# The first block's tile arithmetic on GpSimd, written for VectorE and ScalarE instead

## The chip, the core and the metric

The kernel runs on one core of a Trainium2 chip. A core has TensorE (PE in the profile, its weight loads PEld), VectorE (DVE), ScalarE (ACT), GpSimd (POOL) and SyncE (SP, which here only issues DMAs). The metric is the device time of one execution in microseconds (us); lower is better. The kernel before took 3381.39 us, the median of 3 runs (3380.52 to 3383.11).

## The reference

Two blocks follow each other on a sequence of 1024 tokens of width 1024, in float32.

```python
# first block (one layer)
hx = modulate(rmsnorm(x), sh1, sc1); hc = modulate(rmsnorm(ctx), csh1, csc1)
aq, ak, av, mq, mk, mv, mo, gates = split(h @ w_in)           # for hx and for hc
att = latent_attention(rope(norm(aq)), rope(norm(ak)), av, cak, cav, sink)  # window 128, 8 heads
h_sum = bidir_mlstm(silu(conv(mq)), silu(conv(mk)), mv, ...)  # 4 heads, chunks of 128, two directions
mix = concat([att, rmsnorm(h_sum) * norm_w * sigmoid(mo)])
x = x + g1 * (mix @ w_out)
x = x + g2 * expert_choice_ffn(modulate(rmsnorm(x), sh2, sc2))  # 16 experts, 128 tokens each
# second block: an even layer (pooling, spatial gate) and an odd layer (dilated attention, gated conv), final rmsnorm
return rmsnorm(odd_layer(even_layer(x)))
```

The change touches what stands up to `x = x + g1 * (mix @ w_out)`, and the norm and modulation behind it; here that part is called the mixer. Experts and second block stay as they are.

## The kernel before

A float32 product is made of three matmuls: each operand is split into a high part, rounded to the type fp32r (`hi`, a copy on ACT), and the rest (`lo`, a subtraction), and `mm3` (L156 to L162) adds hi·hi, lo·hi and hi·lo. So weights that arrive from DRAM in `raw` need one cast on ACT (L148) and one subtraction, `lo_sub` (L134 on POOL, L136 on DVE), before TensorE can use them. `wchunk` does both; it takes its engine from `lo_engines`, which `run` sets to `["pool"]` (L204). There are 2 buffers of `raw` and 3 each of `hi` and `lo` in the mixer.

The mixer runs in this order:

- `h_all` (L340): normed rows are transposed, then `finish` (L361) makes hi and lo of `hx`, the modulated input; `kv_tile` projects attention keys, values and gates.
- `keys`, `gates`, `ctx_heads`, `proj_q` (L423 to L683): keys and queries are normed (`qk_norm`, L450), rotated (`rope`, L462), doubled (`qd`, L440 and L675) and transposed. `gates` is a long chain of small DVE instructions (L488 to L606).
- Four mLSTM heads: `head_qk`, `head_vo` project (weights by `wchunk`); `head_states` (L725) walks over the chunks for the states `C`; `head_chunks` (L752) makes, for each of 8 chunks, weights `W = exp(E + g)`, a product, and the normed output `hs` (L786, L787). The mask is added to `E` once for 4 chunks (L767).
- `mod_sums` (L314) adds up the modulation vectors in `macc` (L328, DVE), a DMA of `mraw` for each of its steps, spread between the heads.
- `attention` (L805): the fourth head's chunks run between the first attention blocks. `att_scores` (L891) makes a softmax in `P` for four heads of a group and scales each by `rl` (L933 for the first on POOL, L935 on DVE for the others); `att_values` (L938) transposes and multiplies; `out_tile` (L965) applies `w_out` (weights `wo`, scaled by `g1` at L838), adds the residual, norms and routes.

The program's source doesn't fix the order of the instructions: a scheduler (the tile layer's, with `high_priority` for the chunks) orders them for each engine when the program is built, and each engine then runs its own list strictly in that order. Where an instruction changes its engine, the lists of the others can move as well.

```python
    def lo_sub(self, lo, raw, hi, eng=None):
        ...
        if eng == "pool":
            nc.gpsimd.tensor_sub(lo, raw, hi.bitcast(F32))
        else:
            nc.vector.tensor_sub(lo, raw, hi.bitcast(F32))
```

Of the kernel before, what the change touches and what calls it, by code (L numbers as in the profile page):

```python
# [19 lines left out]
P = 128  # L20
# [62 lines left out]
class K:  # L83
# [115 lines left out]
    def run(self):  # L199
        tc = self.tc  # L200
        with ExitStack() as es:
            self.cpool = es.enter_context(tc.tile_pool(name="const", bufs=1))
            self.dram = es.enter_context(tc.tile_pool(name="dram", bufs=1, space=DRAM))
            self.lo_engines = ["pool"]  # L204
            self.const()
            for ph in (self.mixer, self.moe, self.even, self.odd):
                ph()
                if self.stop == ph.__name__:
                    return
# [131 lines left out]
    def h_all(self):  # L341
        nc, A = self.nc, self.A
        self.hx = ([self.t("hx", [D], F32R, "hxh") for _ in range(KT)], [self.t("hx", [D], F32R, "hxl") for _ in range(KT)])
        hc = [self.t("X", [4, 256], F32R, "hc") for _ in range(4)]
        self.hc = ([hc[k // 4][:, k % 4, :] for k in range(KT)], [hc[2 + k // 4][:, k % 4, :] for k in range(KT)])
        xnT = self.t("xnT", [KT, D])
        self.jtag = "tmp"

        def normed(src, t0, n):
            ts = []  # L350
            ss, rs = self.t("ss", [n]), self.t("ss", [n])
            for i in range(n):
                t = self.t("xin", [D])
                nc.sync.dma_start(t, A[src][(t0 + i) * P:(t0 + i + 1) * P, :])
                ts.append(t)
            self.norm_rows(ts, rs, ss)
            for i in range(n):
                nc.vector.tensor_scalar_mul(ts[i], ts[i], rs[:, i:i + 1])
            return ts

        def finish(h, l, src, kt, a):  # L361
            sc, sh = self.sc1[:, a, kt:kt + 1], self.sh1[:, a, kt:kt + 1]
            tmp = self.t("tmp", [h.shape[-1]])
            nc.scalar.activation(h, src, AF.Identity, scale=sc, bias=sh)  # L364
            nc.vector.tensor_scalar(tmp, src, sc, sh, op0=ALU.mult, op1=ALU.add)
            self.lo_sub(l, tmp, h, ("pool", "dve")[kt % 2])

        for t0 in range(8):
            for t in normed("x", t0, 1):
                for hf in range(2):  # L370
                    ps = self.pt("tr")
                    for k in range(4):
                        kt = hf * 4 + k
                        nc.tensor.transpose(ps[:, k * P:(k + 1) * P], t[:, kt * P:(kt + 1) * P], self.ident)
                    o = xnT[:, hf * 4:hf * 4 + 4, t0 * P:(t0 + 1) * P]
                    pv = ps.rearrange("p (a b) -> p a b", a=4)
                    if hf == 0:
                        nc.scalar.copy(o, pv)
                    else:
                        nc.vector.tensor_copy(o, pv)  # L380
        self.mod_early()
        self.kv_open()
        for hf in range(2):
            s = slice(hf * 512, hf * 512 + 512)
            for kt in range(KT):
                finish(self.hx[0][kt][:, s], self.hx[1][kt][:, s], xnT[:, kt, s], kt, 0)
            for t in range(4):
                self.kv_tile(hf * 4 + t)
        ts = normed("ctx", 0, 2)
        for kt in range(KT):  # L390
            ps = self.pt("tr")
            for i, t in enumerate(ts):
                nc.tensor.transpose(ps[:, i * P:(i + 1) * P], t[:, kt * P:(kt + 1) * P], self.ident)
            finish(self.hc[0][kt], self.hc[1][kt], ps[:, :256], kt, 1)
        for t in range(2):
            self.kv_tile(8 + t)
# [25 lines left out]
    def keys(self):  # L422

        nc, A, mp = self.nc, self.A, self.mp
        kx, kc = self.ktok, self.kct
        self.rt = self.t("rt", [8, 2, 32])
        nc.sync.dma_start(self.rt.rearrange("p t a d -> p (t a d)"), A["cst"][:, CST["rope"]])
        kr = self.t("k", [8, P], name="kr")
        self.qk_norm(kx.rearrange("p a (b c) -> p (a b) c", c=64), 1, kr)
        self.rope(kr, kx, 2)  # L430
        self.qk_norm(kc.rearrange("p a (b c) -> p (a b) c", c=64), 1, self.t("c1", [2, P], name="ksq"))
        self.dump("akr", kr)
        self.dump("kc", kc)
        kcc = mp.tile([P, 4, 256], F32R, name="kcc")
        self.kc = [(kcc[:, 2 * v], kcc[:, 2 * v + 1]) for v in range(2)]
        self.kx = [[mp.tile([P, D], F32R, name=f"kx{v}{i}") for i in range(2)] for v in range(2)]
        for src, t0 in [(kr, t) for t in range(0, 8, 2)] + [(kc, 0)]:
            kd = self.t("qd", [4, 2, 64])
            kv = src[:, t0:t0 + 2].rearrange("p t (v d) -> p (t v) d", v=2)
            nc.gpsimd.tensor_copy(kd, kv[:, :, None, :].to_broadcast([P, 4, 2, 64]))  # L440
            ps = self.pt("tr")
            for v in range(2):
                for t in range(2):
                    c = (v * 2 + t) * P
                    nc.tensor.transpose(ps[:, c:c + P], kd[:, t * 2 + v].rearrange("p a d -> p (a d)"), self.ident)
            for v in range(2):
                o = self.kc[v] if src is kc else [x[:, t0 * P:t0 * P + 256] for x in self.kx[v]]
                self.split2(o[0], o[1], ps[:, v * 256:(v + 1) * 256])

    def qk_norm(self, x, which, sq):  # L450
# [6 lines left out]
        nc.vector.tensor_reduce(ss, sq, axis=AX.X, op=ALU.add)  # L457
        self.rstd(rs, ss, 1.0 / 64)
        nc.vector.tensor_mul(x, x, rs[:, :, None].to_broadcast([P, n, 64]))
        nc.gpsimd.tensor_mul(x, x, self.qkn[:, which:which + 1, :].to_broadcast([P, n, 64]))  # L460

    def rope(self, out, x, nh, t0=0):  # L462

# [6 lines left out]
        o = out.rearrange("p t (h a d) -> p t h a d", a=2, d=32)  # L470
        for i, op in ((0, ALU.subtract), (1, ALU.add)):
            tmp = self.t("rtmp", [nt * nh, 32]).rearrange("p (t h) d -> p t h d", t=nt)
            nc.gpsimd.tensor_mul(o[:, :, :, i], v[:, :, :, i], cos)
            nc.vector.tensor_mul(tmp, v[:, :, :, 1 - i], sin)
            nc.vector.tensor_tensor(o[:, :, :, i], o[:, :, :, i], tmp, op=op)

# [223 lines left out]
    def head_vo(self, h):  # L700
# [6 lines left out]
        for t in range(0, 8, 2):  # L707
# [5 lines left out]
            nc.scalar.activation(so[:, t:t + 2], pv[:, :, 128:256], AF.Sigmoid)  # L713
            if t == 4:
                next(self.mod, None)
        nc.gpsimd.tensor_mul(so, so, nw[:, None, :].to_broadcast([P, 8, P]))
        return vo, so

    def head(self, h, hd):
# [32 lines left out]
    def head_chunks(self, h, hd, C, hook=None):  # L752
# [5 lines left out]
        for c in range(8):  # L758
            if hook:
                hook(c)  # L760
            if c % 4 == 0:

                E = self.t("E", [4, 2, P])
                src = self.mdr.rearrange("(c h) x -> h c x", h=4)[h][c:c + 4]
                ev = E.rearrange("p c d t -> p c (d t)")
                nc.sync.dma_start(ev, src[None].to_broadcast([P, 4, 256]))
                nc.gpsimd.tensor_add(ev, ev, self.mmask[:, None, :].to_broadcast([P, 4, 256]))  # L767
            s = slice(c * P, (c + 1) * P)
            pq = self.pt("s")
            nc.tensor.matmul(pq[:, :P], kT[:, s], qT[:, s], start=True, stop=True)  # L770
# [12 lines left out]
            nc.vector.scalar_tensor_tensor(den[:, 0], it[:, :, 128], -1.0, it[:, :, 128], op0=ALU.mult, op1=ALU.max)  # L783
            nc.vector.tensor_tensor(den[:, 0], den[:, 0], self.flo[:, :, c, h], op=ALU.max)
            nc.vector.reciprocal(den[:, 1], den[:, 0])
            nc.gpsimd.tensor_scalar(hs[:, c], it[:, 0, :P], den[:, 1, 0:1], None, op0=ALU.mult)  # L786
            nc.vector.scalar_tensor_tensor(hs[:, c], it[:, 1, :P], den[:, 1, 1:2], hs[:, c], op0=ALU.mult, op1=ALU.add)  # L787
            pool, n, bufs = self.tags["hj"]
            junk = pool.tile([P, P], BF16, tag="hj", name=self.nm("hj"), bufs=bufs)
# [2 lines left out]
        rs = self.t("hss", [8])  # L792
        self.rstd(rs, ss, 1.0 / P, "hrst")
        nc.vector.tensor_mul(hs, hs, rs[:, :, None].to_broadcast([P, 8, P]))
        nc.gpsimd.tensor_mul(hs, hs, so)
        for hf in range(2):
            ps = self.pt("tr")
            for t in range(4):
# [6 lines left out]
    def attention(self, last, right):  # L805
        nc, A, tc = self.nc, self.A, self.tc
        with ExitStack() as es:
# [3 lines left out]
            self.open(hp, "m2h", {"C3": (2080, 1), "kt3": (512, 2), "kw3": (128, 3)})  # L811
            self.banks(es, "m2l", {"sl": 1, "sc": 1, "O": 1})
            self.sls = ["sl"]
            self.npool = 1
            self.am = self.t("am", [640])
            nc.sync.dma_start(self.am[:, :384], A["cst"][:, CST["amask"]])
            nc.gpsimd.memset(self.am[:, 384:], 0.0)
# [15 lines left out]
            def weights(c, tag):  # L833
                hi, lo = self.t(tag, [2, D], F32R), self.t(tag, [2, D], F32R)
                for k in range(2):
                    raw = self.t("x1", [D])
                    nc.sync.dma_start(raw, A["wout"][c][:, k * D:(k + 1) * D])
                    nc.gpsimd.tensor_mul(raw, raw, g1)  # L838
                    nc.scalar.copy(hi[:, k], raw)
                    self.lo_sub(lo[:, k], raw, hi[:, k], "dve" if c > 1 else "pool")  # L840
                    self.wo.append((hi[:, k], lo[:, k]))

            def hook(c):
# [51 lines left out]
    def att_scores(self, v, b):  # L895
# [33 lines left out]
        nc.vector.tensor_add(l, l, es)  # L929
        nc.vector.reciprocal(rl, l)  # L930
        for g in range(4):
            if g < self.npool:
                nc.gpsimd.tensor_scalar(Ps[g], Ps[g], rl[:, g:g + 1], None, op0=ALU.mult)  # L933
            else:
                nc.vector.tensor_scalar_mul(Ps[g], Ps[g], rl[:, g:g + 1])  # L935
        return Ps
# [28 lines left out]
    def out_tile(self, b, at):  # L965
# [3 lines left out]
        raw, hm = self.t("hraw", [4, P]), self.t("hm", [2, 4, P], F32R)  # L969
        nc.sync.dma_start(raw, self.mixT.rearrange("(k p) t -> p k t", p=P)[:, :, r])  # L970
        nc.scalar.copy(hm[:, 0], raw)
        nc.gpsimd.tensor_sub(hm[:, 1], raw, hm[:, 0].bitcast(F32))
        m = [(at[0][:, k], at[1][:, k]) for k in range(4)] + [(hm[:, 0, k], hm[:, 1, k]) for k in range(4)]
        x = self.t("x1", [D])
        nc.sync.dma_start(x, A["x"][r, :])
# [22 lines left out]
        self.norm_rows([x], rs, ss)  # L998
        h2 = self.t("h2", [D])
        nc.vector.scalar_tensor_tensor(h2, x, rs, self.scb, op0=ALU.mult, op1=ALU.mult)  # L1000
        nc.gpsimd.tensor_add(h2, h2, self.shb)
        store(self.h2d[r, :], h2)
        st, lg, ex = self.t("sm", [4]), self.t("sm", [16]), self.t("sm", [16])
        nc.vector.scalar_tensor_tensor(lg, pl, rs, self.rsh, op0=ALU.mult, op1=ALU.add)
# [921 lines left out]
```

## Time and profile before

| | |
|---|---|
| median of 3 runs | 3381.39 us (3380.52 to 3383.11) |
| the profiled execution | 3381.84 us, of which the span from first to last instruction is 3379.7 us |
| busy: PE, DVE, ACT, POOL | 92%, 60%, 40%, 44% of the span |
| mean granted TensorE clock | 0.96 of full speed |
| the mixer | from 0 to about 803.5 us of the span |
| routing, experts | about 803.5 to 1180 us, then the second block |

The profile gives, for each engine, the time in which an instruction ran. Groups of instructions have one line each: line of the source, engine, operation, what it writes and reads, shapes and count, then busy time and mean duration of one in ns, then the idle time of the engine before them and what ended it. A wait is put down to the instruction that ended it last. [...]

### The profile page before, as it was taken

How to read it: one execution, taken by the hardware profiler on the slowest of the kernel's cores; microseconds unless marked ns; L12 is line 12 of the kernel's file. 1: busy time of each engine (PE TensorE's matmuls, PEld its weight loads, DVE VectorE, ACT ScalarE, POOL GpSimd, SP SyncE). 2: the span in 40 equal slices, each digit the busy share in tenths (PEclk: the TensorE clock that was granted, in tenths of full speed). 3: DMA queues.
4: the chain of work that ended last, by engine and by line, in shares of the span. 5: the costliest groups of instructions: out<-in, count | busy, mean ns of one | idle time of the engine just before them, and what ended most of it. 6: DMA issues, size and time to landing. Idle time of an engine off the chain costs nothing. (4 is left out here: it accounts for less than half of the span.)

```text
span 3379.7 us, 43941 instructions
## 1 busy us (share of the span) xinstructions
PE 3111.2 (92%) x15829; PEld 2570.3 (76%) x15829; DVE 2037.8 (60%) x3777; ACT 1367.7 (40%) x2509; POOL 1480.0 (44%) x1010
## 2 busy tenths in 40 slices
PE   6798888997999769999998899999999999999998
PEld 4787675776777668787786788888888888877777
DVE  5676677766799864555556555455455456444445
ACT  4445445453778643333312434334334333232312
POOL 2443242422232354456654434334334334566673
PEclk8899988998999979999998899999999999999999
DMA  5233321427999522112441111111111111122342
GB/s 196 70 125 101 113 72 38 137 100 279 373 376 383 170 81 75 63 63 75 172 124 69 34 48 46 50 49 46 47 47 48 47 44 51 54 72 69 103 153 75
DMA packets 142877, 366.76 MB, mean 109 GB/s; under 512 B 17298, under 2 KB 27058, under 8 KB 142660
## 3 DMA queue, kind: packets, MB, share of 16 engines
q1 hardware_dynamic: 137764, 346.14, 29.5%
q0 software_dynamic: 4896, 17.83, 2.1%
q8 instruction: 124, 2.03, 0.2%
q14 instruction: 93, 0.76, 0.1%
HBM read 311.43 MB, written 52.48 MB: 108 GB/s over the span
## 5 line engine op out<-in xcount | busy, mean ns | idle before, releaser
L1264 PE MATMUL ps_mm<-h,hi 128*128 128x512 f32 (+1 forms) x4272 | 1090.6, 395 | 42.4 <-ACT qk L1292 10.8
L1264 PEld LDWEIGHTS ps_mm<-h,hi 128*128 128x128 f32 x4272 | 786.2, 190 | 213.0 <-ACT qk L1292 17.2
L134 POOL TENSOR_TENSOR lo<-S,hi 128x512 fp32r<-128x512 f32 x302 | 402.8, 1337 | 586.5 <-PE ps_mm L1264 396.5
L134 POOL TENSOR_TENSOR lo<-raw,hi 128x512 fp32r<-128x512 f32 (+2 forms) x274 | 412.3, 1509 | 371.3 <-ACT hi L1196 231.9
L1264 PE MATMUL ps_mm<-h,lo 128*128 128x512 f32 (+1 forms) x2136 | 567.5, 389 | 0.0
L1264 PEld LDWEIGHTS ps_mm<-h,lo 128*128 128x128 f32 x2136 | 400.7, 190 | 82.5
L1196 ACT CAST hi<-S 128x512 fp32r<-128x512 f32 x302 | 187.1, 620 | 536.2 <-PE ps_mm L1264 514.6
L1196 ACT CAST hi<-raw 128x512 fp32r<-128x512 f32 x240 | 149.0, 622 | 368.5 <-PE ps_mm L1264 319.9
L148 ACT CAST hi<-raw 128x1024 fp32r<-128x1024 f32 (+1 forms) x222 | 230.8, 1049 | 93.0 <-PE ps_mm L162 63.8
L136 DVE TENSOR_TENSOR lo<-raw,hi 128x1024 fp32r<-128x1024 f32 x188 | 247.1, 1340 | 34.1 <-ACT hi L148 28.1
L1217 DVE TENSOR_TENSOR S<-raw,raw 128x512 f32<-128x512 f32 x76 | 66.6, 877 | 201.8 <-POOL lo L134 200.6
L160 PE MATMUL ps_mm<-hi,hxh 128*128 128x256 f32 (+1 forms) x448 | 132.3, 297 | 9.2 <-ACT hxh L364 5.4
L162 PE MATMUL ps_mm<-hi,hxl 128*128 128x256 f32 (+1 forms) x448 | 131.1, 294 | 1.3 <-POOL hxl L134 1.3
L161 PE MATMUL ps_mm<-lo,hxh 128*128 128x256 f32 (+1 forms) x448 | 131.3, 294 | 0.0
L1183 POOL TENSOR_TENSOR y<-y,g 128x1024 f32<-128x1024 f32 x15 | 40.2, 2680 | 204.7 <-ACT y L1179 179.3
L1213 DVE TENSOR_TENSOR S<-S,raw 128x512 f32<-128x512 f32 x76 | 102.4, 1347 | 39.0 <-POOL lo L134 38.8
L161 PE MATMUL ps_mm<-lo,xT 128*128 128x512 f32 x256 | 105.4, 412 | 14.5 <-DVE lo L136 13.2
L1294 DVE TENSOR_TENSOR qk<-ps_mm,pq 128x512 f32<-128x512 f32 (+1 forms) x75 | 69.1, 940 | 68.8 <-PE ps_mm L1264 68.5
L1745 DVE CUSTOM_DVE_ANT_0 P<-ps_s,bias 128x128 f32<-128x128 f32 (+1 forms) x192 | 61.8, 348 | 80.4 <-PE ps_s L1740 78.7
L160 PE MATMUL ps_mm<-hi,xT 128*128 128x512 f32 x256 | 104.0, 406 | 2.8 <-ACT hi L148 2.6
L134 POOL TENSOR_TENSOR yl<-r,yh 128x1024 fp32r<-128x1024 f32 x28 | 68.5, 2447 | 82.1 <-ACT yh L1365 82.1
L162 PE MATMUL ps_mm<-hi,xT 128*128 128x512 f32 x256 | 101.8, 398 | 0.2
(590 smaller groups left out, 6523.2 us busy)
## 6 DMA issues: line engine op xcount, KB each, us to landing
raw<-in_wexp_dram SPq DMA_DIRECT2D x192, 512.0 KB
raw<-in_wo_dram SPq DMA_DIRECT2D x228, 256.0 KB
mraw<-in_wmod_dram SPq DMA_DIRECT2D x64, 256.0 KB
raw<-in_we_dram SPq DMA_DIRECT2D x64, 256.0 KB
r<-ye SPq DMA_DIRECT2D x14, 512.0 KB
r<-in_weo_dram SPq DMA_DIRECT2D x14, 512.0 KB
r<-yo SPq DMA_DIRECT2D x14, 512.0 KB
r<-in_wo_dram SPq DMA_DIRECT2D x14, 512.0 KB
```

What stands on the lines that cost most here:

```text
L134: nc.gpsimd.tensor_sub(lo, raw, hi.bitcast(F32))
L136: nc.vector.tensor_sub(lo, raw, hi.bitcast(F32))
L148: self.nc.scalar.copy(hi, raw)
L160: nc.tensor.matmul(out, l[0], r[0], start=start, stop=False)
L161: nc.tensor.matmul(out, l[0], r[1], start=False, stop=False)
L162: nc.tensor.matmul(out, l[1], r[0], start=False, stop=stop)
L1196: self.nc.scalar.copy(hi, x)
L1213: nc.vector.tensor_sub(s2, s1, a11)
L1217: nc.vector.tensor_sub(s3, a11, a21)
L1264: nc.tensor.matmul(ps, w[a][:, kt * P:(kt + 1) * P], h[b][:, kt, cs], start=start and i == 0, stop=i == 11, skip_group_check=True)
L1294: self.nc.vector.tensor_add(dst, ps, add)
L1745: nc.vector.tensor_tensor_reduce(p, ps, bias[:, n - m:], op0=ALU.add, op1=ALU.max, scale=1.0, scalar=-3e38, accum_out=mx[:, j:j + 1])
```

## The change

Every arithmetic instruction on tiles that the mixer gave to POOL is written for DVE or ACT. On POOL there stay only memsets and DMA issues until the experts begin. To DVE go: all `lo` subtractions (30 of weight chunks, 4 of `wo`, 8 of `hxl`, 4 of `hc`, 8 of `hm`), the mask additions (8), the norm weights of q and k (6), one product of each rotation (10), the gate products (`so` 4, `hs` 4), the scalings of `w_out` by `g1` (8) and the shifts of `h2` (8). To ACT go: the first scaling of a chunk's `hs` (32, as a Copy with a scale), the first group's scaling of `P` (16), and the doubled keys (5 copies).

```diff
-            self.lo_engines = ["pool"]
+            self.lo_engines = ["dve"]
...
-            self.lo_sub(l, tmp, h, ("pool", "dve")[kt % 2])
+            self.lo_sub(l, tmp, h, "dve")
...
-            nc.gpsimd.tensor_copy(kd, kv[:, :, None, :].to_broadcast([P, 4, 2, 64]))
+            nc.scalar.copy(kd, kv[:, :, None, :].to_broadcast([P, 4, 2, 64]))
...
-        nc.gpsimd.tensor_mul(x, x, self.qkn[:, which:which + 1, :].to_broadcast([P, n, 64]))
+        nc.vector.tensor_mul(x, x, self.qkn[:, which:which + 1, :].to_broadcast([P, n, 64]))
...
-            nc.gpsimd.tensor_mul(o[:, :, :, i], v[:, :, :, i], cos)
+            nc.vector.tensor_mul(o[:, :, :, i], v[:, :, :, i], cos)
...
-        nc.gpsimd.tensor_mul(so, so, nw[:, None, :].to_broadcast([P, 8, P]))
+        nc.vector.tensor_mul(so, so, nw[:, None, :].to_broadcast([P, 8, P]))
...
-                nc.gpsimd.tensor_add(ev, ev, self.mmask[:, None, :].to_broadcast([P, 4, 256]))
+                nc.vector.tensor_add(ev, ev, self.mmask[:, None, :].to_broadcast([P, 4, 256]))
...
-            nc.gpsimd.tensor_scalar(hs[:, c], it[:, 0, :P], den[:, 1, 0:1], None, op0=ALU.mult)
+            nc.scalar.activation(hs[:, c], it[:, 0, :P], AF.Copy, scale=den[:, 1, 0:1])
...
-        nc.gpsimd.tensor_mul(hs, hs, so)
+        nc.vector.tensor_mul(hs, hs, so)
...
-                    nc.gpsimd.tensor_mul(raw, raw, g1)
+                    nc.vector.tensor_mul(raw, raw, g1)
...
-                    self.lo_sub(lo[:, k], raw, hi[:, k], "dve" if c > 1 else "pool")
+                    self.lo_sub(lo[:, k], raw, hi[:, k], "dve")
...
-                nc.gpsimd.tensor_scalar(Ps[g], Ps[g], rl[:, g:g + 1], None, op0=ALU.mult)
+                nc.scalar.activation(Ps[g], Ps[g], AF.Copy, scale=rl[:, g:g + 1])
...
-        nc.gpsimd.tensor_sub(hm[:, 1], raw, hm[:, 0].bitcast(F32))
+        nc.vector.tensor_sub(hm[:, 1], raw, hm[:, 0].bitcast(F32))
...
-        nc.gpsimd.tensor_add(h2, h2, self.shb)
+        nc.vector.tensor_add(h2, h2, self.shb)
```

`moe` sets `lo_engines` to `["pool"]` itself before it uses it, so the experts' subtractions stay where they were.

How the lists of two engines move is seen at two places. First DVE in the stage of `keys` and `gates`, where `gt` (L497) is the polynomial at the head of the gates' chain, `kT` a context head's convolution and `rst` a norm's small steps. Before:

```order
L612 TENSOR_SCALAR kT_1272<-uc_1271,colv 128x256
L178 RECIPROCAL rst_938<-rst_938 128x4
L497 SCALAR_TENSOR_TENSOR gt_1013<-gt_1013,gt_1011 128x80
L613 SCALAR_TENSOR_TENSOR kT_1272<-uc_1271,colv,kT_1272 128x256
L179 TENSOR_TENSOR rst_938<-rst_938 128x4
```

And now:

```order
L136 TENSOR_TENSOR lo_1387<-raw_1384,hi_1386 128x1024
L475 TENSOR_TENSOR kr_910<-kr_910,rtmp_925 128x16x32
L475 TENSOR_TENSOR kr_910<-kr_910,rtmp_929 128x16x32
L497 SCALAR_TENSOR_TENSOR gt_1013<-gt_1013,gt_1011 128x80
L180 TENSOR_TENSOR rst_938<-rst_938 128x4
L614 SCALAR_TENSOR_TENSOR kT_1312<-uc_1311,colv,kT_1312 128x256
L136 TENSOR_TENSOR lo_1427<-raw_1424,hi_1426 128x1024
```

The weights' subtractions `lo_1387` and `lo_1427`, which stood on POOL, now stand on DVE in front of the gates' polynomial, which has moved behind the rotation of the keys.

Second ACT in the chunks of the second head (`hs_3449`), where `W` is the exponential of the mask, `it` the scaled state product, `hj` the squares for the norm and `so` the output gate of the next head:

```order
 L780 ACTIVATE it_3485<-ps_s_3484,decc_1165 128x130 x2
+L786 ACTIVATE hs_3449<-it_3462,den_3469 128x128
 L773 ACTIVATE W_3551<-E_3546,g_1054 128x128 x2
 L790 ACTIVATE hj_3475,hss_3450<-hs_3449 128x128
+L780 ACTIVATE it_3508<-ps_s_3507,decc_1165 128x130 x2
+L713 ACT_TABLE_LOAD
+L713 ACTIVATE so_3878<-ps_mm_3882 128x256
+L786 ACTIVATE hs_3449<-it_3485,den_3492 128x128
+L790 ACTIVATE hj_3498,hss_3450<-hs_3449 128x128
```

The scaling L786 stands in ACT's list between a chunk's other steps, and once behind a load of another function table.

## Rows read from the trace of the kernel before

**Rows 1.** Busy time by stage; `us` is the stage, (x) counts, then clock and DMA
```profile
core 0: us, PE busy (x) PEld busy (x) DVE busy (x) ACT busy (x) POOL busy (x), PEclk, DMA share, GB/s
0.00:803.50 803.50, 684.85 (x4255) 564.33 (x4255) 543.41 (x1391) 368.85 (x762) 283.25 (x178) 0.91 0.33 108
160.00:232.00 72.00, 68.67 (x472) 63.00 (x471) 58.05 (x85) 37.59 (x66) 38.08 (x18) 0.98 0.26 87
470.00:590.00 120.00, 94.33 (x496) 69.78 (x495) 96.43 (x328) 63.88 (x176) 47.99 (x33) 0.79 0.21 66
590.00:803.50 213.50, 199.94 (x1140) 150.91 (x1138) 144.47 (x397) 94.33 (x194) 69.49 (x34) 0.96 0.39 127
```

**Rows 2.** Groups of POOL's instructions, 0 to 803.5 us
```profile
L134 POOL TENSOR_TENSOR lo<-raw,hi 128x1024 fp32r<-128x1024 f32 x28 | 70.2, 2513 | 60.0 <-ACT hi L148 50.7 <-PE ps_mm L331 5.4 <-issue 3.0
L786 POOL TENSOR_SCALAR hs<-it,den 128x128 f32<-128x128 f32 x32 | 19.8, 622 | 94.0 <-DVE den L785 70.5 <-ACT it L780 6.5 <-DVE ast L930 5.0
L767 POOL TENSOR_TENSOR E<-E,mmask 128x1024 f32<-128x1024 f32 x8 | 19.0, 2375 | 45.1 <-DMA E<-mdr 30.3 <-issue 14.8
```

**Rows 3.** Groups of DVE's instructions, 0 to 803.5 us
```profile
L328 DVE SCALAR_TENSOR_TENSOR macc<-mraw,csil,macc 128x512 f32<-128x512 f32 x64 | 66.8, 1044 | 38.0 <-DMA mraw<-in_wmod_dram 31.0 <-DMA macc<-in_brow_dram 6.1 <-issue 0.4
L935 DVE TENSOR_SCALAR P<-P,ast 128x640 f32<-128x640 f32 x36 | 27.9, 825 | 0.1
L787 DVE SCALAR_TENSOR_TENSOR hs<-it,den,hs 128x128 f32<-128x128 f32 x32 | 15.4, 482 | 23.2 <-POOL hs L786 23.0
L475 DVE TENSOR_TENSOR qr<-qr,rtmp 128x512 f32<-128x512 f32 x8 | 15.1, 1911 | 0.0
L745 DVE TENSOR_SCALAR kw<-ps_tr,ws 128x128 f32<-128x128 f32 x42 | 13.9, 343 | 1.0 <-PE ps_tr L733 1.0
L745 DVE TENSOR_SCALAR kw<-kt,ws 128x128 f32<-128x128 f32 x14 | 10.9, 784 | 1.3 <-ACT kt L736 1.3
L474 DVE TENSOR_TENSOR rtmp<-q,rt 128x512 f32<-128x512 f32 x8 | 9.6, 1236 | 4.6 <-POOL q L460 4.5
L136 DVE TENSOR_TENSOR hxl<-tmp,hxh 128x512 fp32r<-128x512 f32 x8 | 5.4, 679 | 0.1
L136 DVE TENSOR_TENSOR wo<-x,wo 128x1024 fp32r<-128x1024 f32 x4 | 4.9, 1219 | 0.7 <-ACT wo L839 0.7
```

**Rows 4.** Timeline: DVE and POOL side by side around 336 us, and 614 us
```profile
333.55 5.29 POOL L134 TENSOR_TENSOR lo<-raw,hi 128x1024 fp32r<-128x1024 f32 x2 [3.01 <-issue]
336.43 2.96 DVE L328 SCALAR_TENSOR_TENSOR macc<-mraw,csil,macc 128x512 f32<-128x512 f32 x1
...
349.70 0.75 DVE L328 SCALAR_TENSOR_TENSOR macc<-mraw,csil,macc 128x512 f32<-128x512 f32 x1 [0.42 <-DMA mraw<-in_wmod_dram]
...
614.15 1.47 DVE L935 TENSOR_SCALAR P<-P,ast 128x640 f32<-128x640 f32 x3
```

**Rows 5.** Groups of ACT's instructions, 0 to 803.5 us
```profile
L928 ACT ACTIVATE P<-P,ast 128x640 f32<-128x640 f32 x48 | 39.2, 819 | 21.7 <-DVE ast L924 21.5
L713 ACT ACT_TABLE_LOAD x12 | 15.4, 1283 | 6.2 <-DVE vo L712 6.1
L790 ACT ACTIVATE hj<-hs 128x128 bf16<-128x128 f32 x32 | 9.8, 308 | 41.0 <-DVE hs L787 31.6 <-DVE ast L924 5.8 <-DVE den L783 3.5
L675 ACT COPY qd<-qr 128x512 f32<-128x512 f32 x16 | 9.7, 623 | 15.4 <-DVE qr L475 15.4
```

**Rows 6.** Waits of PE, 0 to 803.5 us: total, times, longest
```profile
PE ps_mm L298 <- DMA hi<-in_wmod_dram: 13.9, 4, 8.6
PE ps_mm L160 <- ACT hi L148: 8.6, 2, 8.2
PE ps_mm L331 <- DVE macc L328: 7.8, 1, 7.8
PE ps_sl L914 <- DVE ast L918: 7.5, 5, 2.0
PE ps_s L779 <- DVE W L774: 6.9, 4, 4.1
PE ps_mm L161 <- POOL lo L134: 5.2, 2, 4.3
```

More of the change, by code (lines that the diff above doesn't have):

```diff
@@ L813, in attention @@
             self.sls = ["sl"]
-            self.npool = 1
+            self.nact = 1
             self.am = self.t("am", [640])
@@ L931, in att_scores @@
         for g in range(4):
-            if g < self.npool:
-                nc.gpsimd.tensor_scalar(Ps[g], Ps[g], rl[:, g:g + 1], None, op0=ALU.mult)
+            if g < self.nact:
+                nc.scalar.activation(Ps[g], Ps[g], AF.Copy, scale=rl[:, g:g + 1])
             else:
```

## The prediction

> **What bounds the kernel now.** I read four things in this order: busy times by stage, the groups of POOL and DVE with the idle time before them, the timeline where the two engines run at once, and PE's waits. In the mixer, 803.5 us, PE is busy for 684.85 us and idle for 118.65 us; DVE is busy for 543.4 us (68%), ACT for 368.9 us (46%), POOL for 283.25 us (35%) [rows 1]. So PE is the longest resource, and no gain at the same clock can exceed its 118.65 us of idle time. Nor is DVE free everywhere: in the stage of the fourth head's end and the first attention blocks (470 to 590 us) it is busy for 96.4 of 120 us, while PE is busy for 94.3, and the granted clock there is 0.79, against 0.96 in the stage after it [rows 1]. Between 160 and 232 us DVE is busy for 58.05 of 72 us [rows 1].
>
> The groups show POOL slow at its work: a weight's `lo` takes 2.51 us, the same shape on DVE 1.22 us (`wo`) [rows 2, 3]. They also show DVE's instructions unequal. `macc` takes 1.044 us on average, yet 0.75 us where nothing runs beside it, and 2.96 us where POOL's `lo` does [rows 3, 4]. Three `P` scalings behind each other took 1.47 us, 0.49 each, against a mean of 0.825 [rows 3, 4]. So the price of POOL's work is partly paid on DVE.
>
> [...]
>
> PE's waits say where that could matter. Three of the largest end with a DVE instruction: `macc` 7.8, `ast` 7.5 and `W` 6.9 us, together 22.2 us. POOL's `lo` ended 5.2 us, ACT's `hi` 8.6, and a DMA of modulation weights 13.9 us [rows 6]. The rest of PE's idle time lies in many smaller pieces.
>
> **Work added to DVE.** Of width 1024 come 30 chunks' `lo`, 4 of `wo`, 8 mask additions, 4 `so`, 4 gate products `hs`, 8 scalings by `g1` and 8 shifts: 66 x 1.219 = 80.5 us by the `wo` row [rows 3]. Of width 512 come 8 `hxl`, 8 `hm`, 6 norm weights and 10 rotation products: 32 x 0.679 = 21.7 us by the `hxl` row. Four `hc` at half of that are 1.4 us. Sum 103.6 us.
>
> **Time DVE gets back.** If POOL no longer runs beside it, six groups shrink to their unshared durations [rows 3, 4]: `macc` 66.8 - 64 x 0.75 = 18.8 us; `P` 27.9 - 36 x 0.49 = 10.3; `qr` 15.1 - 8 x 0.679 = 9.7; `kw` from `kt` 10.9 - 14 x 0.343 = 6.1; `rtmp` 9.6 - 8 x 0.679 = 4.2; `hs` L787 15.4 - 32 x 0.343 = 4.4. That is 53.5 of their 145.7 us, 37%. The unshared duration of `kw` and of `hs` is taken from the 128x128 row that reads PSUM, the nearest there is. DVE's net load grows by 103.6 - 53.5 = 50 us, to some 593 us of 803.5.
>
> **The sum, term by term.**
> T1, the chunk's `hs`. The first scaling goes from 0.622 us on POOL to about 0.308 us on ACT, by the row of `hj`, the same width [rows 2, 5]: 32 x 0.314 = 10.0 us out of a chain in which DVE waited 23.0 us for POOL [rows 3]. The chain stands between a chunk's product and its norm, not always in front of PE; I take half, **-5** (bounds 0 and -10).
> T2, the stretched links. PE waits 22.2 us on DVE in the three rows; 37% of that is **-8** (bounds 0 and -53.5, the whole stretch on the path).
> T3, the weights. PE waits 5.2 us for `lo` [rows 6], which becomes 1.22 of 2.51 us: 5.2 x 0.51, **-3** (bounds 0 and -5.2).
> T4, DVE's added load. Nearly all of the net 50 us lies in DVE's 260 us of idle time (803.5 - 543.4). The three waits of 22.2 us per 543.4 us of DVE work are 4%; 4% of 50 is **+2** (bounds 0 and +50).
> T5, ACT. 32 x 0.308 + 16 x 0.819 + 5 x 0.623 + 2 further table loads x 1.283 = 28.7 us [rows 5], so ACT goes from 369 to 398 us, half of the stage. By the same rule, 8.6 us of waits per 368.9 us, it costs **+1** (bounds 0 and +28.7). Behind each such Copy stand the next `it`, `W` and `qd` in ACT's list.
> POOL's DMA issues lose the arithmetic in front of them; the work that they feed waits for other things in the rows, so 0 (bounds 0 and -13.9, the wait on modulation weights). Experts and second block are not touched: 0.
>
> The sum is -13 us against the profiled 3381.84 us, which lies 0.45 us above the median of the runs: **3368 us** on the median. Its own range is 3355 to 3377. What can be told from no change is about 0.2%, 6.8 us, so 3374.6 to 3388.2 counts as the same.
>
> **What speaks against the change.** DVE runs its list strictly in order. A `lo` that waits on POOL delays only POOL; on DVE it delays everything behind it. POOL waited 50.7 us for ACT's `hi` in front of `lo`, and 30.3 us for the DMA of `E` in front of the mask [rows 2]. The new list puts two weights' `lo` ahead of or among the gates' polynomial and the rotation of the keys, and the addition of the mask stands before a chunk's `W`, for which PE already waits 6.9 us [rows 6]. While a `lo` waits there, ACT keeps working only as far as it needs nothing of DVE.
>
> **The rivals.**
> B, a larger gain. DVE is the pacemaker of the latency chains (gates, chunks, softmax), and half of the 53.5 us of stretch lies on them: -27, with T1 and T3 at their bounds, -10 and -5, that is -42: 3340 us. For it: stage 470 to 590, with DVE busier than PE and the clock at 0.79 [rows 1]; were PE to wait less and be granted 0.96 there, its 94.3 us alone would shrink by 94.3 x (1 - 0.79/0.96) = 17 us. Against it: the listed waits on DVE are only 22.2 us.
> C, no change. PE's idle time is led by DMAs and by the order of its own list; what comes early waits for PE, and all five terms vanish: 3381, within 6 us. For it: PE busy 200 of 213.5 us behind 590 us [rows 1], and the DMA wait of 13.9 us [rows 6]. That the change doesn't do what it says is part of this: the program could be short of POOL work but still stretched by DMAs' own writes.
> D, slower: DVE inherits POOL's waits. If half of the 50.7 + 30.3 = 81.0 us becomes idle time of DVE on the path, that is +40, with the sum of -13 a net +27: 3408 us. It decides from 13 us on, a sixth of the 81. For it: the new places of `lo` in front of the gates. Against it: DVE has other work ahead of most of these places, which gives the awaited `hi` and DMA time to land, and the scheduler may put the waiting instruction later.
> E, slower, no relief: the stretch has another cause than POOL. Then the 103.6 us come in full, and by POOL's busy shares 48.0/283.25 and 38.1/283.25 some 17.5 and 14 us of them fall into the two stages in which DVE is the busiest engine or near it [rows 1]. If all of it lands, less T1 and T3, that is +23: 3404 us. The row with 2.96 against 0.75 us speaks against it [rows 4].
> [...]
>
> **How the numbers follow.** Forecast A 0.45, B 0.18, C 0.16, D 0.16, E 0.05. D gets as much as C because two inherited waits of 81 us stand against a gain of 13. Faster by over 0.2%: 0.40 of A, all of B, 0.02 of C, 0.60 in all. Same: 0.05 of A, 0.13 of C, 0.02 of D, 0.20. Slower: 0.20, from D, E and 0.01 of C. The range, 3337 to 3405 us, leaves out the lower part of B (0.08) and the upper part of D and E (0.10).
>
> **What would show it.** T2 is right if `macc` comes down to about 0.75 us, `P` to 0.49 and `qr` to 0.68, and if PE's waits on `macc`, `ast` and `W` shrink together from 22.2 to about 14 us. T1 is right if DVE's 23.0 us of waits in front of L787 fall by about 10. T3: PE's waits on `lo` fall from 5.2 to 2 or 3 us. T4: DVE busy near 593 us in the mixer. T5: ACT near 398 us, with no new wait of PE on ACT. D would be seen as idle time of DVE in front of L136 and L767, ended by ACT's `hi` and by the DMA of `E`; the forecast is wrong if that exceeds some 13 us and PE's idle time grows with it. E would be seen as `macc` still near 1.04 us; C as a mixer still 803 us long with shorter DVE groups.

## The result, and the profile after

The changed kernel took 3335.71 us, the median of 4 runs (3330.76 to 3336.12), against 3381.82 us of 4 runs of the kernel before on the same chip: ratio 0.986, 95% interval 0.9846 to 0.9873. That is 46 us faster, where 13 were forecast; the range began 1.3 us above it. The mixer ends at 758.4 us of the span instead of 803.5, both taken where the first weight load of L1108 starts; what follows it kept its length (3334.3 - 758.4 = 2575.9 us, 3379.7 - 803.5 = 2576.2 before).

Busy time by stage in the changed kernel, columns as in [rows 1]. The first row stops 1.4 us before the mixer's end. The second row runs from 45 us to the end of the queries (the last `qhl`, 206.6 us).

```profile
0.00:757.00 757.00, 674.98 (x4254) 554.75 (x4254) 529.47 (x1489) 395.42 (x815) 6.93 (x23) 0.93 0.36 114
45.00:206.60 161.60, 156.25 (x1167) 148.00 (x1167) 135.07 (x348) 92.61 (x169) 0.88 (x5) 0.98 0.29 95
470.00:590.00 120.00, 103.99 (x594) 73.90 (x594) 98.22 (x317) 70.90 (x168) 0.00 (x0) 0.90 0.31 95
```

The stage of keys, gates and queries in the kernel before, 45 us to its last `qhl`, and a part of it:

```profile
45.00:239.70 194.70, 166.60 (x1178) 156.90 (x1177) 142.84 (x307) 88.67 (x162) 88.91 (x54) 0.90 0.24 78
88.00:160.00 72.00, 55.33 (x416) 52.99 (x416) 48.05 (x149) 29.57 (x57) 35.15 (x24) 0.86 0.26 81
```

So 33 of the 46 us were gained by the end of the queries. PE's busy time there fell by 10 us with the granted clock at 0.98 instead of 0.90, its idle time by 23 us (28.1 to 5.4). Over the mixer PE's idle time fell from 118.65 us to 82. DVE took over 103.6 us of work by the prediction's count, and yet was busy for 529.5 us instead of 543.4 [rows 1]: it got back 543.4 + 103.6 - 529.5 = 117.5 us, not 53.5. Counted by the durations of single instructions, what came to DVE took 106 us and what it got back is 106 us too; the prediction's six groups gave 54 of these, as forecast, and groups that it left out gave the other half.

The rest of the gain can be placed by the ends of the heads' last norm (L794): the first head became 11 us shorter, the second 1 and the third 8. What stands behind the third head's norm, the fourth head and the attention, became 8 us longer, with 24 matmuls more behind that mark; before, then changed:

```profile
530.00:803.50 273.50, 253.58 (x1466) 187.76 (x1466) 190.81 (x564) 126.97 (x280) 86.09 (x48) 0.94 0.33 108
477.10:758.40 281.30, 261.25 (x1490) 193.80 (x1490) 197.07 (x604) 143.97 (x319) 1.90 (x3) 0.94 0.32 105
```

Groups of DVE's instructions in the changed mixer, beside [rows 3]:

```profile
L328 DVE SCALAR_TENSOR_TENSOR macc<-mraw,csil,macc 128x512 f32<-128x512 f32 x64 | 48.0, 749 | 23.7 <-DMA mraw<-in_wmod_dram 18.2 <-DMA macc<-in_brow_dram 5.1
L136 DVE TENSOR_TENSOR lo<-raw,hi 128x1024 fp32r<-128x1024 f32 (+1 forms) x30 | 36.8, 1225 | 4.1 <-ACT hi L148 3.9
L935 DVE TENSOR_SCALAR P<-P,ast 128x640 f32<-128x640 f32 x36 | 17.8, 549 | 0.1
L787 DVE SCALAR_TENSOR_TENSOR hs<-it,den,hs 128x128 f32<-128x128 f32 x32 | 11.2, 349 | 10.8 <-ACT hs L786 10.6
L767 DVE TENSOR_TENSOR E<-E,mmask 128x1024 f32<-128x1024 f32 x8 | 9.8, 1226 | 17.5 <-DMA E<-mdr 17.5
L475 DVE TENSOR_TENSOR qr<-qr,rtmp 128x512 f32<-128x512 f32 x8 | 5.4, 680 | 0.1
L745 DVE TENSOR_SCALAR kw<-ps_tr,ws 128x128 f32<-128x128 f32 x42 | 14.0, 346 | 4.2 <-PE ps_tr L733 4.2
L745 DVE TENSOR_SCALAR kw<-kt,ws 128x128 f32<-128x128 f32 x14 | 3.9, 282 | 1.4 <-ACT kt L736 1.4
L612 DVE TENSOR_SCALAR kT<-uc,colv 128x256 f32<-128x256 f32 x4 | 1.4, 344 | 0.0
L497 DVE SCALAR_TENSOR_TENSOR gt<-gt,gt 128x80 f32<-128x80 f32 x7 | 1.7, 243 | 0.0
```

Two short groups that the prediction did not count, as they were before:

```profile
L497 DVE SCALAR_TENSOR_TENSOR gt<-gt,gt 128x80 f32<-128x80 f32 x7 | 7.6, 1088 | 0.1
L612 DVE TENSOR_SCALAR kT<-uc,colv 128x256 f32<-128x256 f32 x4 | 5.4, 1354 | 1.0 <-ACT uc L641 1.0
```

`macc`, `P` and `qr` came down to what the prediction said: 0.749 us, 0.49 us of busy time each (17.8 / 36) and 0.680 us. The inherited waits are small: 3.9 us in front of `lo`, 17.5 in front of `E`. PE's waits:

```profile
PE ps_mm L298 <- DMA hi<-in_wmod_dram: 15.0, 4, 9.1
PE ps_sl L914 <- DVE ast L918: 6.3, 7, 1.7
PE ps_s L779 <- DVE W L774: 4.5, 5, 1.5
...
PE ps_mm L331 <- DVE macc L328: 2.8, 1, 2.8
...
PE ps_mm L161 <- DVE lo L136: 2.0, 2, 1.0
```

The three DVE rows fell from 22.2 to 13.6 us, as T2 said (14), and PE's waits on `lo` from 5.2 to 2.0, as T3 said. Those two terms came true on the rows that they were made from, 12 us, and most of the gain lay elsewhere. In the query stage PE's waits that ACT ended fell from 15.3 us to nothing and those that POOL ended from 6.5 to nothing, while those that DVE ended stayed (4.5 and 5.0 us). The largest of them, 8.6 us for ACT's `hi` [rows 6], had been left alone by the sum. This is what stood behind it, in the timeline of the kernel before (DVE, POOL, then ACT and PE):

```profile
107.51 7.04 DVE L497 SCALAR_TENSOR_TENSOR gt<-gt,gt 128x80 f32<-128x80 f32 x4
114.48 2.43 DVE L612 TENSOR_SCALAR kT<-uc,colv 128x256 f32<-128x256 f32 x1
...
107.32 2.36 POOL L460 TENSOR_TENSOR kx<-kx,qkn 128x1024 f32<-128x1024 f32 x1 [3.03 <-DVE uc L639]
109.64 2.34 POOL L134 TENSOR_TENSOR lo<-raw,hi 128x1024 fp32r<-128x1024 f32 x1
111.94 2.51 POOL L473 TENSOR_TENSOR kr<-kx,rt 128x512 f32<-128x512 f32 x2
114.41 2.34 POOL L134 TENSOR_TENSOR lo<-raw,hi 128x1024 fp32r<-128x1024 f32 x1
...
118.16 0.42 ACT L615 ACTIVATE kT<-kT 128x256 f32<-128x256 f32 x1 [7.36 <-DVE kT L614]
...
121.07 0.42 ACT L615 ACTIVATE kT<-kT 128x256 f32<-128x256 f32 x1 [2.49 <-DVE kT L614]
121.39 1.03 ACT L148 CAST hi<-raw 128x1024 fp32r<-128x1024 f32 x1
...
122.48 0.58 PE L160 MATMUL ps_mm<-hc,hi 128*128 128x256 f32 x1 [8.21 <-ACT hi L148]
```

Read from the bottom: PE waits 8.21 us for a `hi`. ACT casts it at once after `kT`, which stands ahead of it in ACT's list and waited 7.36 us and 2.49 us for DVE. DVE at that time ran four steps of the gates' polynomial in 7.04 us, one for each POOL instruction that ran beside them (each step ended 0.1 us after its POOL instruction), and then one `kT` of 2.43 us beside a `lo`. In the changed kernel such a polynomial step takes 0.24 us and that `kT` 0.34. PE's wait carries ACT's name, and its cause is POOL's work, through DVE.

### The profile page after: what moved, and what is told of

It is laid out like the page before. It is cut to its first block, busy times and chain, and to the rows that moved or that the text cites. A ratio compares the mean times of both kernels' runs of the same rounds, so it can differ in the third digit from the quotient of the medians.

```text
span 3334.3 us, 43810 instructions
## 1 busy us (share of the span) xinstructions
PE 3098.8 (93%) x15829; PEld 2559.3 (77%) x15829; DVE 2026.3 (61%) x3879; ACT 1394.8 (42%) x2564; POOL 1206.4 (36%) x855
## 5 line engine op out<-in xcount | busy, mean ns | idle before, releaser
L1264 PE MATMUL ps_mm<-h,hi 128*128 128x512 f32 (+1 forms) x4272 | 1088.6, 394 | 44.7 <-ACT qk L1292 10.8
L134 POOL TENSOR_TENSOR lo<-raw,hi 128x512 fp32r<-128x512 f32 (+1 forms) x244 | 337.4, 1387 | 313.0 <-ACT hi L1196 232.8
L136 DVE TENSOR_TENSOR lo<-raw,hi 128x1024 fp32r<-128x1024 f32 (+1 forms) x218 | 285.0, 1330 | 35.5 <-ACT hi L148 31.7
L160 PE MATMUL ps_mm<-hi,xT 128*128 128x512 f32 x256 | 103.8, 405 | 2.4 <-ACT hi L148 2.1
L1365 ACT CAST yh<-r 128x1024 fp32r<-128x1024 f32 x28 | 29.4, 1050 | 180.5 <-PE ps_s L161 168.5
```

The lines of the kernel that those rows point to most:

```text
L160: nc.tensor.matmul(out, l[0], r[0], start=start, stop=False)
L1264: nc.tensor.matmul(ps, w[a][:, kt * P:(kt + 1) * P], h[b][:, kt, cs], start=start and i == 0, stop=i == 11, skip_group_check=True)
```

## The experiments

Each ratio is to the kernel before on the same chip. The changed kernel itself was run again beside the others, 0.9869 (0.9852 to 0.9885):

> The changed kernel once more, unaltered, as the measure beside which the other kernels of this call stand on the same chip: ratio to the kernel before 0.986 as first measured. What the single parts lose is read against it.

A difference of two ratios is uncertain by about 0.0023, or 8 us. The losses and gains below are differences to this 0.9869, where no other kernel is named; the first measurement, 0.986, would make losses 3 us larger and gains 3 us smaller. For smaller differences the end of the query stage in the profile is given as well, which moved by 1 us between the changed kernel's two profiles; the mixer's end moved by 4.

**The weights' `lo` alone, and all but them.**

```diff
-            self.lo_engines = ["dve"]
+            self.lo_engines = ["pool"]
```

> The changed kernel with one thing undone: the 30 weight chunks' lo subtractions are on POOL again; all else stays on DVE and ACT. Theory W (weights' feed): most of the 46 us came from here. In the kernel before, PE waited in the stage of keys, gates and queries (45 to 181 us) 8.6 us for hi, 5.2 us for POOL's lo and 3.8 us for kx, and each slow lo also held one of the two raw buffers, so that the next weight's transfer and its hi came late; W expects over half of the gain to be lost, 3360 to 3366 us, and PE waits on hi and lo of 10 us or more in the mixer. Rival S (stretch everywhere): the gain is DVE's relief from POOL, in proportion to POOL's busy time; 75 of 283 us of POOL work come back, so a quarter of the gain is lost, about 12 us: 3348 us.

Measured: 0.9932 (0.9913 to 0.995), 3360.6 us: 21 us lost. The query stage ends at 222.6 us, 16 later, and holds 41.1 us of POOL work. The converse edit on the kernel before:

> The kernel before with one part of the change alone: the 30 weight chunks' lo subtractions on DVE, all else as before. W: over half of the gain is there with this part alone, 3352 to 3357 us, and the time of the last qhl (end of the query stage) falls from 239.7 us to about 215. S: a quarter of the gain, about 3370 us. Third theory Q (DVE's queue): with POOL still at work beside it, DVE is stretched and inherits the waits for hi; no gain or a loss, 3380 us or more.

Measured: 0.9942 (0.9921 to 0.9964), 3366.2 us: 20 us gained; query stage 225.0 us. Both agree: the 30 subtractions are worth 20 us, somewhat under half of the gain, between W and S; Q, a loss, falls.

**The other groups back on POOL.** First the keys' steps (L440, L460, L473):

> The changed kernel with the norm weights of q and k, the rotation products and the doubled keys on POOL again (21 instructions); the weights' lo stay on DVE. Theory K (the keys' chain): the stage of keys and queries, which became 33 us shorter by its end, was held by POOL's and DVE's alternating steps of norm and rotation, so some 15 to 20 us are lost: 3351 to 3356 us. W: the weights' feed is the cause and not this chain, so at most 5 us are lost: up to 3341 us. S: about 30 of 283 us of POOL work, 5 us: 3341 us.

Measured: 0.9873 (0.9853 to 0.9893): 1 us on the whole, though the query stage ends 7.5 us later (214.1). K falls for the time, holds in part for the stage. Then the attention's pieces (L838, half of L840, L933, L972, L1001):

> The changed kernel with the attention's pieces on POOL again: first group's P scaling (16), scalings of w_out by g1 (8), half of the wo subtractions (4), hm (8) and the shift of h2 (8). The run with hs back showed that a move to ACT can cost time. If the same holds for P, the time is at or below the changed kernel's, 0 to 10 us less. S: some 80 of 283 us of POOL work come back, 12 us more. The prediction's own terms gave these pieces no more than 2 us either way.

Measured: 0.9881 (0.9865 to 0.9898), 4 us, within the uncertainty. The heads' pieces (L716, L767, L795):

> The changed kernel with the heads' DMA-fed and gate pieces on POOL again: mask additions to E (8), products so (4) and hs by so (4). DVE then no longer waits 17.5 us for the DMA of E. If DVE's inherited wait (the prediction's rival D) costs time inside the changed kernel, the time falls by 5 us or more. S: some 38 of 283 us of POOL work come back, 6 us more; and W's place, E, stands before the exponential of a chunk, where POOL took 2.4 us for 1.2.

Measured: 0.9867 (0.985 to 0.9883), no difference: the 17.5 us for which DVE waits for `E` cost nothing that can be seen. Last, these two groups together with `hs`:

> The changed kernel with hs, the attention's pieces (P, g1, half of wo, hm, h2) and the heads' pieces (E, so, hs by so) all on POOL again; moved stay only the weights' lo, hxl and hc and the keys' steps. One group at a time, these changed the time by -13, +4 and -1 us. If parts add: 10 us less than the changed kernel, ratio to the kernel before 0.984. If a POOL with much to do costs more than its parts (its own queue, DVE beside it all the time): 5 us more or over, ratio 0.9885 or above.

Measured: 0.9878 (0.9863 to 0.9893), 3 us more, where the sum of the parts would have been 10 less. That the groups do not add is not shown by this: a sum of three differences and the run beside it are together uncertain by some 16 us.

Beside the run with `lo` alone, this run tells where the rest of the gain is. The two kernels differ by `hxl`, `hc` and the keys' steps, which are off POOL here and on it there; everything of the heads and the attention is on POOL in both. They lie 0.0064 apart, 22 us with an uncertainty of 9, and 19 us at the end of the query stage (225.0 and 205.9 us):

```profile
45.00:225.00 180.00, 163.43 (x1174) 154.93 (x1173) 139.10 (x322) 92.19 (x167) 47.86 (x38) 0.93 0.26 86
45.00:205.90 160.90, 155.50 (x1165) 147.36 (x1164) 134.91 (x347) 92.08 (x167) 0.88 (x5) 0.98 0.30 95
```

So with POOL's work gone up to the end of the queries, all but 3 us of the gain are there, to which `hs` on POOL adds its part (below). Which of these steps brings the 22 us stays open, since the keys' steps alone, put back, cost 1 us.

**POOL at work beside DVE, with nobody waiting for it.** In the changed kernel, up to the query stage:

```diff
             nc.vector.tensor_sub(lo, raw, hi.bitcast(F32))
+            if eng == "dve" and self.beside:
+                nc.gpsimd.tensor_copy(self.js[:, 0:1], lo[:, 0:1].bitcast(F32))
+                nc.gpsimd.tensor_sub(self.js, self.js, self.js)
+                nc.gpsimd.tensor_sub(self.js, self.js, self.js)
```

> The changed kernel with work on POOL that nobody waits for: behind each of the 16 weight subtractions of the stages of keys, gates and queries (all on DVE) POOL runs two subtractions of width 512 on a tile of its own, about 2.6 us each pair, some 42 us in all up to 200 us; the lists of PE, DVE and ACT are word for word those of the changed kernel. S (stretch: DVE is slowed by POOL's mere running): the end of the query stage, 206.6 us, moves out by 10 us or more, of the 16 us that it moves when the lo itself is on POOL; DVE's instructions that lie beside POOL's take two to four times as long. W (weights' feed: what cost time is that the lo came late and held raw): the end of the query stage moves by 4 us at most, and so does the whole time.

Measured: 0.9891 (0.9874 to 0.9907), 7 us slower; the query stage ends at 217.4 us, 10.8 later. The stage of this kernel, and its rows of POOL's work and of the polynomial (line 508 here is L497):

```profile
45.00:217.40 172.40, 160.52 (x1178) 151.62 (x1179) 151.29 (x352) 93.56 (x169) 41.03 (x45) 0.96 0.28 91
```

```profile
L139 POOL TENSOR_TENSOR js<-js 128x512 f32<-128x512 f32 x16 | 20.4, 1274 | 1.3
```

```profile
L508 DVE SCALAR_TENSOR_TENSOR gt<-gt,gt 128x80 f32<-128x80 f32 x7 | 4.1, 591 | 0.0
```

With the same lists, DVE's busy time rose from 135.07 to 151.29 us by 41 us of POOL work, and the polynomial's steps from 0.243 to 0.591 us. The stage grew by 10.8 us, 0.67 us for each of DVE's 16.2. In this trace nothing waits for POOL up to that point, and every DMA there is issued by SP. This is S, shown without any wait for POOL. It was repeated on the kernel with `hs` on DVE (below):

> The kernel with hs on DVE, and POOL's superfluous 42 us beside the 16 weight subtractions; the lists of PE, DVE and ACT are word for word those of the kernel with hs on DVE without it (0.9837 of the kernel before). If the price of stretch is real and not a chance of one order of the lists, it repeats here: query stage out by 9 to 12 us (207.4 us without), 7 to 10 us on the whole, ratio 0.986 to 0.9867. If it was given back later by chance or not: ratio within 0.001 of 0.9837.

Measured: 0.9858 (0.9843 to 0.9873) against 0.9837, again 7 us; stage end 218.1 against 207.4 us, 10.7 later, with DVE busy 16.4 us longer (151.49 against 135.09). One difference of 7 us alone lies within the uncertainty; two that agree, each with the stage's end, do not.

**DVE itself at work.** The same lines with `nc.vector` for `nc.gpsimd`:

> The changed kernel with the same superfluous work as in the run with work beside, but on DVE itself: behind each of the 16 weight subtractions up to the query stage two subtractions of width 512 on a tile of its own (32 x 0.68 us, 16 small copies, some 23 us in all). Beside POOL's 42 us DVE's own instructions up to 206.6 us had grown by 17.6 us and the stage by 10.8 us. Theory P (DVE's time is what the stage is made of: every us on DVE costs it over half a us, whatever makes it): the end of the query stage moves out by 10 us or more, the whole time by 7 to 14 us. The prediction's term T4 (added DVE work costs 4% of itself): 1 us.

Measured: 0.9869 (0.9854 to 0.9885), no loss, though the stage ends 8.2 us later (214.8). The added work took 24.1 us, 19.5 of them behind 45 us, yet the stage's row has DVE busy only 11.8 us longer:

```profile
45.00:214.80 169.80, 157.42 (x1153) 148.22 (x1153) 146.88 (x380) 91.76 (x166) 0.84 (x5) 0.95 0.28 91
```

So some 8 us of other DVE work moved out of the stage: the scheduler ordered the lists anew. By DVE's busy time the stage is 0.7 us longer for each us, as with stretch; by the work that was added it is 0.34. Whether the loss would reach the end in another order was asked on the kernel with `hs` on DVE:

> The kernel with hs on DVE, and the 23 us of superfluous work on DVE itself behind the same 16 subtractions (here the scheduler orders the other lists anew, as it did in the run without hs moved, where the query stage came 7.3 us later and the whole time stayed). If DVE's added work is covered behind the stage (the prediction's T4, 1 us): ratio 0.983 to 0.9845. If the missing loss was a chance of the order: ratio 0.986 or above, 7 us more.

Measured: 0.9864 (0.9849 to 0.9879) against 0.9837: 9 us lost, stage end 215.6 us, again 8.2 later. P's 10 us for the stage were not reached either time, and its 7 us for the whole time once of two.

**The two steps given to ACT.** First the scaling L786 back on POOL:

```diff
-            nc.scalar.activation(hs[:, c], it[:, 0, :P], AF.Copy, scale=den[:, 1, 0:1])
+            nc.gpsimd.tensor_scalar(hs[:, c], it[:, 0, :P], den[:, 1, 0:1], None, op0=ALU.mult)
```

> The changed kernel with the first scaling of the chunks' hs (32 instructions) on POOL again. The prediction's term T1 said 5 us (bounds 0 and 10): 3341 us, at most 3346, with DVE waiting some 20 us for POOL's hs again against 10.6 us for ACT's. S: 20 of 283 us of POOL work, 3 us: 3339 us. If the chain of the chunks sets the end in more places than the prediction took, over 10 us: above 3346 us.

Measured: 0.9829 (0.9811 to 0.9847), 3326.1 us: faster than the changed kernel by 10 to 13 us, against every theory. Then on DVE:

> The changed kernel with the first scaling of the chunks' hs on DVE instead of ACT. With it on POOL the kernel was about 0.4% faster than the changed one. Theory A (ACT's list is what costs: on ACT the scaling waits 19.3 us for den and everything behind it waits with it): 6 to 12 us are gained here as well, 3327 to 3333 us on a chip where the kernel before takes 3382. Theory O (POOL was the right place because it is free, and both other engines are full): 0 to 5 us lost, 3336 to 3341 us.

Measured: 0.9837 (0.9823 to 0.985), 3328.3 us, 11 us gained. POOL and DVE serve equally, and ACT cost time. ACT's rows in the changed mixer, and in the kernel with `hs` on DVE that step and the ones behind it:

```profile
L786 ACT ACTIVATE hs<-it,den 128x128 f32<-128x128 f32 x32 | 12.6, 399 | 19.3 <-DVE den L785 19.3
L790 ACT ACTIVATE hj<-hs 128x128 bf16<-128x128 f32 x32 | 9.8, 306 | 12.0 <-DVE hs L787 12.0
```

```profile
L787 DVE SCALAR_TENSOR_TENSOR hs<-it,den,hs 128x128 f32<-128x128 f32 x32 | 11.2, 349 | 0.6
L786 DVE TENSOR_SCALAR hs<-it,den 128x128 f32<-128x128 f32 x32 | 9.1, 284 | 0.7
L790 ACT ACTIVATE hj<-hs 128x128 bf16<-128x128 f32 x32 | 9.9, 309 | 38.5 <-DVE hs L787 38.4
```

On ACT it takes 0.399 us and waits 19.3 us for `den`, and DVE then 10.6 us for it; `den`, L786 and L787 are one chain, and on DVE it runs through with 0.6 us of idle time. That these hand-overs, or what they hold up in ACT's list, are the cost is not shown: with `hs` on DVE, ACT idles longer in front of this chain's steps (38.5 us against 19.3 + 12.0), and with `hs` on POOL, DVE still waits 8.9 us in front of L787. The scheduler also ordered PE's, DVE's and ACT's lists otherwise from about 270 us on, a rival that no run separates. In the profiles of these two kernels the stretch from the third head's last norm to the mixer's end takes 273 and 276 us, against 281 in the changed kernel and 280 in its second profile. Whether the cost lies there was asked with the fourth head alone:

> The changed kernel with that scaling on POOL for the fourth head alone, whose chunks run between the first attention blocks (8 of 32 instructions); the other heads' stay on ACT. With all 32 on POOL the heads' ends were where the changed kernel has them (first three heads within 1.5 us) and the gain of about 10 us came behind 480 us. If the cost is ACT's busy stage of the fourth head and the attention: 7 to 12 us gained, as with all 32. If it is spread over the heads: a quarter, 2 to 3 us.

Measured: 0.9855 (0.984 to 0.987), 5 us gained, between the two theories and within the uncertainty of both. Then `P` too was taken from ACT, with `nact` 0 and `hs` on POOL, then on DVE:

> A candidate: the changed kernel with hs on POOL (0.9829 of the kernel before) and the first group's scaling of P on DVE, so that the change gives ACT neither of its two new steps. If ACT's list is the cost for P as it was for hs: another 3 to 6 us, ratio 0.981 to 0.982. If DVE is the fuller engine in the attention: 16 x 0.53 us more on it, ratio 0.983 to 0.985.

Measured: 0.983 (0.9817 to 0.9844), 3328.9 us.

> A candidate: hs and P both on DVE, POOL free of arithmetic. With hs alone on DVE the ratio was 0.9837. If ACT's list is the cost for P too: 0.982 to 0.983. If DVE is the fuller engine in the attention, where it is busy for over 80%: 0.984 to 0.986.

Measured: 0.9828 (0.9814 to 0.9841), 3327.5 us. `P` on ACT or on DVE makes no difference that can be told. With `hs` off ACT all four kernels lie at 0.983 to 0.984, 55 to 58 us faster than the kernel before and 8 to 14 faster than the changed one, by which of its two measurements is taken. In the profiles of the last two the stretch behind the third head takes 279 and 278 us, so where `hs` on ACT costs its time stays open too.

## Why the prediction was wrong

The side was right and the size was not: 13 us were forecast and 46 came. By its steps:

- **T2, the stretched links, is the step that failed.** It took 37% of "22.2 us" of PE's waits, the three largest rows that a DVE instruction ended, and set the time DVE gets back at 53.5 us of six groups. Both were too narrow. All rows that DVE ended make 59.3 us, and the waits that vanished in the query stage carried the names of ACT and POOL (21.8 us) and not DVE's. DVE got back about twice the 53.5 us, since the gates' polynomial, the convolutions and other short groups were stretched too: L497 took 1.09 us on average before and 0.243 after, L612 1.35 and 0.344. PE's wait of 8.6 us for ACT's `hi` was stretch of DVE two links back. The stage where this chain lies gave 33 us. By the two runs with superfluous work on POOL, stretch cost this stage 0.65 to 0.67 us for each us by which DVE was busy longer, or 10.8 us for 40 us of POOL work; for the 88 us of POOL work that left the stage that is, as an estimate, 24 of the 33 us. T2 had 8 for the whole mixer. The prediction read the stages at 160 and 470 us and not the one at 88 to 160 us, where the polynomial stands and PE was idle for 16.7 of 72 us.
- **T3, the weights**, was taken as -3. The 30 subtractions were worth 20 us. By the run with work beside, 41 us of POOL work cost the query stage 10.8 us by stretch alone, of the 16 that it loses with `lo` on POOL. But there DVE does the 16 subtractions as well. In the run with `lo` back DVE is spared them and is busy only 7.1 us longer in the stage (142.21 us): at 0.67 that explains 5 of the 16 us, and some 11 are left for POOL's late `lo` and the other order of the lists. This split is worked out, not shown.
- **T4, the added load**, had the wrong sign in its size: DVE's net load fell by 14 us instead of rising by 50. Its price, 4%, was too low for the stage (8.2 us for 24 us of work), and for the whole 0 in one order of the lists and 9 us in another.
- **T1 and T5, ACT.** T1's chain got shorter where it was looked for (DVE's waits in front of L787 from 23.0 to 10.6 us, with 0.399 us for a scaling instead of 0.308), and T5's busy time was right, 395 us against 398. But `hs` on ACT costs 8 to 14 us against DVE or POOL, where the two terms together said -4. Why it costs that is open, and ACT's busy share, by which T5 was priced, did not show it.
- **Rival B** was the nearest, 3340 us, and by its mechanism: stretch on latency chains, and clock given back (0.90 to 0.98 in the query stage). But it looked for the effect between 470 and 590 us, and it came in the queries. That the clock between 470 and 590 us rose from 0.79 to 0.90 says less than it seems, since other work stands there now; the stretch from the third head's last norm to the mixer's end got no shorter.
- **Rival D** fell: DVE inherited 3.9 + 17.5 = 21.4 of the 81.0 us of waits, and the larger part of these, at `E`, costs nothing that can be seen when it is put back on POOL. E fell with `macc` at 0.749 us, C with the mixer at 758.

What stays open is how the gain of the query stage divides between stretch and operands that came late from POOL, and why `hs` on ACT costs what it does.

## What to carry to other kernels

Work on POOL beside a DVE that was busy for 68% of the mixer was not free here: some 276 us of POOL work cost DVE about as much time (106 us by single instructions, 117.5 by busy time) as DVE needed to do most of it itself (106 and 103.6 us). When a wait of PE carries another engine's name, follow that engine's list back until an instruction is found that took longer than its kind does elsewhere, and price the wait there. And an engine with time to spare isn't for that reason the right place for a step in the middle of another engine's chain: on ACT, busy for 46% of the mixer before, the scaling of `hs` cost 8 to 14 us.

## What the runs showed of the hardware

Four polynomial steps on DVE took 7.04 us beside four POOL instructions in the kernel before, and each ended 0.1 us after the POOL instruction beside it; in the changed kernel, where POOL has no arithmetic in the mixer, a step takes 0.24 us. The polynomial has two tiles of SBUF as input; `kT` and `P`, with one tile and a column of factors, were stretched as well (2.43 against 0.34 us, 0.825 against 0.549).

The other side shows when the instructions of the kernel before are sorted by whether POOL worked beside them. `kw` made from PSUM took 0.343 us in the 10 cases with POOL's work beside it and in the 32 without. `kw` made from a tile in SBUF, the same operation and shape, took 1.07 us in 9 cases beside POOL's work and 0.28 us in 5 without. Why the one is held up and the other is not, no run here shows.
